# A state-space scan on one core: its two token tiles taken stage by stage in turn, one sum moved from GpSimd to VectorE, one product from VectorE to ScalarE

## The chip, the cores and the metric

The program runs on one core of a Trainium2 chip. Its time is device microseconds of one execution; of three runs of the kernel before the median is 2680.12 us (2672.77 to 2683.09). One execution was also recorded by the hardware profiler, and every row below comes from that one.

## What is computed

Four layers work on 256 context tokens and 256 latent tokens of width 1024: gated linear attention, a state-space mixer (SSD), an even attention mixer and an odd one, each followed by a feed-forward part (the last one a mixture of eight experts). The change is inside the SSD mixer, the second of the four. Cut to the scan, per group of four heads:

```
cum  = cumsum(dt * a)
seg  = cum[:, None] - cum[None, :]
decay = exp(where(mask, seg, -inf))
xdt  = xi * dt
cb   = einsum('bign,bjgn->bijg', ci, bi)
y    = einsum('bijg,bijgr,bjgrp->bigrp', cb, decay, xdt)
y    = y + einsum('bign,bigr,bgrpn->bigrp', ci, exp(cum), s)
```

It runs forwards and backwards over the tokens, the two results are added, `xs * d` is added, and the sum is multiplied by `silu(z)`. There are eight groups. The context's tokens only leave a state; results are wanted for the latents alone.

## The kernel before

Products are made in single precision from split operands: `split` (L419, L420) casts the upper bits on ScalarE and takes the rest on VectorE or GpSimd, and `mm3` (L441 to L443) makes three matmuls of each. A weight unit is loaded by DMA, split in halves of 1024 columns (`whi` on ScalarE at L419, `wlo` on VectorE at L420) and used by `gemm_ws`, where the weights stay and 512 or 256 tokens move.

`ssd` runs one group after another. `gemm(g)` makes the inputs of group g: two units of x (512 tokens each), B (512 tokens), C and two of z (256 tokens each). Each of the first four goes from PSUM through `conv` (L1193 and L1196 on ScalarE, four passes at L1198 on VectorE) into the tile `FZ`; z is copied there at L1212. `scan(g)` starts with SiLU over all of `FZ` (L1220, with a table load ahead of it), so it can't start before all of `gemm(g)` has been evacuated. Then, in steps that end at each `yield`:

- four steps that transpose the four token tiles (L1229), copy them out of PSUM (L1230, ScalarE) and scale x (L1233, VectorE);
- two steps, one per direction, that make the states (L1240, L1248 on TensorE; L1242 ScalarE; L1246, L1251 VectorE; L1250 GpSimd);
- five steps for latent tile 2 and then the same five for tile 3: C times B (L1258) and its two masked copies `gm` (L1262); `R`, a mask times the decay's exponent, as a high part on VectorE and a low part on GpSimd (both L1269), which TensorE sums to `pe` (L1274); `exp(pe)` on ScalarE (L1284), the step sizes times `gm` (`w4`, L1286 ScalarE, L1287 VectorE), and their product `e4` on GpSimd (L1288); the state's part `pi` (L1292), scaled on VectorE (L1294), its two directions added on GpSimd (L1296); last `py` (L1301 and L1304), which needs both that sum and `e4`, then L1307 on VectorE and the product with `silu(z)` on GpSimd (L1310);
- one step that squares the group's result (L1317, ScalarE) and adds it up (L1318, GpSimd).

That is 17 steps. `weave(scan(g), gemm(g + 1), *PACE[2])` takes 1.3 of the next group's gemm steps after each scan step, and what is left of them at the end; the last group is woven with the first products of w_out (`early`, `PACE[3]`, also 1.3). A gemm here has 18 steps (four per x unit, four for B, two for C, two per z unit). So 18 gemm steps are used up after 14 of the scan's 17.

The order on each engine is set when the program is built: a scheduler goes by the program's order, the buffers and its own estimates. Every engine then takes its instructions strictly in that order. Two kinds of buffers matter: `pat` holds two PSUM banks, used in turn for `pg` (C times B), `pe`, `pi` and `py`; `R` has three buffers, two of which one direction of one tile takes. `hc4` is scratch: `w4`, `e4`, and from column 1024 the state's part.

Of the kernel before, what the change touches and what calls it, by code (L numbers as in the profile page):

```python
# [22 lines left out]
# ---------------------------------------------------------------- host layout  # L23
# [43 lines left out]
def _ev_bias(rpb):  # L67
    """Relative position bias by query and key, with the column window's -1e30: [8, 128, 2 * 256]."""
# [22 lines left out]
def _col(v):  # L91
    """[n * 128] -> [128, n]."""
# [3 lines left out]
def _ada_tiles(L, c):  # L96
    """The feature tiles of the conditioning's group c; the first layer's shift and scale come in halves."""
# [39 lines left out]
def layout(inp):  # L137
    """The arrays the program takes; every one a rearrangement of an input or a constant."""
# [20 lines left out]
    # GLA  # L159
# [19 lines left out]
    # SSD  # L179
# [9 lines left out]
    # second block  # L189
# [55 lines left out]
    # constants of the shapes  # L245
# [24 lines left out]
# ---------------------------------------------------------------- the program  # L270
# [11 lines left out]
# steps of filler, and of the conditioning, per step of a phase's main part  # L282
PACE = (0.7, 0.3), (0.45, 0.6), (1.3, 0.3), (1.3, 0.6), (0.9, 0.5), (0.65, 0.5), (0.25, 0.3), (1.25, 0.5), (0.26, 0.3)
# [29 lines left out]
class Net:  # L313
# [10 lines left out]
    def banks(self, mm, tp, at=0, sc=0):  # L324
        """PSUM of a phase: accumulators, transposes, and two kinds for the mixers."""
# [62 lines left out]
    def open_h(self, es):  # L388
        """The residual, tokens on partitions: two tiles of the context, two of the latents."""
# [32 lines left out]
    def load(self, ap, n):  # L422
        """A unit of weights, split, in two halves: w(o, n) = parts of the columns o .. o + n."""
# [14 lines left out]
    def mm3(self, ps, a, b, first, last):  # L438
        """ps += a.T @ b."""
# [5 lines left out]
    def ws_acc(self, w, nm, m, x, t0, nt, ps):  # L445
        """Yields every 3072 columns or so."""
# [5 lines left out]
    def gemm_ws(self, ap, x, evac, nm=2, span=None):  # L452
        """Weights stationary: a unit of nm * 128 columns, tokens moving; evac(m, psum [columns, tokens])."""
# [8 lines left out]
    def gemm_ws_halves(self, units, x):  # L462
        """Several units at once, the context's tokens first: units = [(ap, nm, evac)]."""
# [14 lines left out]
    def gemm_xs(self, units, x, tts, n, evac, fill=0):  # L478
        """Tokens stationary: units = [(ap, ks)], each n columns of the weights of the k-tiles ks."""
# [22 lines left out]
    def unit(self, w, ks, x, pss, first, last, evac=None):  # L502
        """Part of a product with tokens stationary: pss = {token tile: psum}; w(k) the weights of k-tile k, split."""
# [8 lines left out]
    def flush(self):  # L512
        """What was put off until the tensor engine has other work behind it."""
# [1785 lines left out]
```

## Time and profile before

| | |
|---|---|
| median of 3 runs | 2680.12 us |
| the runs | 2672.77, 2683.09, 2680.12 us |
| span of the profiled execution | 2672.4 us |
| run nearest to that span | 2672.77 us, 0.4 us above it |
| TensorE, VectorE, ScalarE, GpSimd busy | 94%, 73%, 46%, 25% of the span |
| the eight scans | from about 831 to 1166 us |

The profiled execution's own time, as the device counts it, is not listed apart; its span agrees with the fastest run to 0.4 us, and 2672.8 us is used for it. A group's scan starts where its transposes (L1229) start: at 831.16, 873.39, 917.40, 963.05, 1007.60, 1052.23, 1097.19 and 1139.13 us. The seven stretches between them are called periods; what follows 1139.13 is the last group, without a next one to weave in. A granted clock of 1.00 is 2.4 GHz, 0.50 is 1.2 GHz.

### The profile page before, as it was taken

How to read it: one execution, taken by the hardware profiler on the slowest of the kernel's cores; microseconds unless marked ns; L12 is line 12 of the kernel's file. 1: busy time of each engine (PE TensorE's matmuls, PEld its weight loads, DVE VectorE, ACT ScalarE, POOL GpSimd, SP SyncE). 2: the span in 40 equal slices, each digit the busy share in tenths (PEclk: the TensorE clock that was granted, in tenths of full speed). 3: DMA queues.
4: the chain of work that ended last, by engine and by line, in shares of the span. 5: the costliest groups of instructions: out<-in, count | busy, mean ns of one | idle time of the engine just before them, and what ended most of it. 6: DMA issues, size and time to landing. Idle time of an engine off the chain costs nothing.

```text
span 2672.4 us, 38317 instructions
## 1 busy us (share of the span) xinstructions
PE 2524.6 (94%) x14350; PEld 2065.7 (77%) x14350; DVE 1962.1 (73%) x3015; ACT 1239.3 (46%) x1899; POOL 659.3 (25%) x533
## 2 busy tenths in 40 slices
PE   6999999999999989899999999999999898999998
PEld 3877668877777777778988877888888676888886
DVE  3566787799988777877566457756438776999987
ACT  2433444223246555545544344322225444878775
POOL 1122334032332333424224123112124431000000
PEclk8999999999999989998999999999999998999999
DMA  8334556665642222245553225555524125999995
GB/s 283 125 129 142 195 200 205 213 219 198 209 161 94 71 67 71 71 159 173 189 188 122 78 71 174 180 194 194 191 92 163 61 72 193 341 328 356 336 334 217
DMA packets 137506, 471.66 MB, mean 176 GB/s; under 512 B 16544, under 2 KB 21792, under 8 KB 137056
## 3 DMA queue, kind: packets, MB, share of 16 engines
q1 hardware_dynamic: 131264, 458.34, 50.8%
q10 hardware_dynamic: 6048, 10.80, 1.2%
q8 instruction: 115, 1.88, 0.3%
q14 instruction: 79, 0.65, 0.1%
HBM read 467.96 MB, written 1.11 MB: 176 GB/s over the span
## 4 chain that ended last, share of the span: by engine, by line
PE 52%; DVE 8%; issue 4%; POOL 3%; ACT 2%; DMA 0%; ACTq 0%; DVEq 0%; POOLq 0%
PE b L441 15%; PE b L443 15%; PE b L442 15%; DVE wlo L420 2%; DVE FZ L1198 1%; PE b L1396 1%; POOL hrs L1371 1%; POOL Hc L1296 1%; PE b L1427 1%; PE b L1415 1%; DVE R L1269 1%; PE b L1301 1%; ACT whi L419 1%; PE b L1930 1%; PE b L2007 1%
## 5 line engine op out<-in xcount | busy, mean ns | idle before, releaser
L419 ACT ACTIVATE whi<-wraw 128x1024 fp32r<-128x1024 f32 x472 | 491.9, 1047 | 582.4 <-PE b L443 246.6
L420 DVE TENSOR_TENSOR wlo<-wraw,whi 128x1024 fp32r<-128x1024 f32 x472 | 594.4, 1268 | 209.0 <-ACT whi L419 205.4
L441 PE MATMUL b<-whi,big 128*128 128x512 f32 (+1 forms) x1696 | 600.1, 355 | 5.6 <-DVE xn L1374 4.1
L442 PE MATMUL b<-wlo,big 128*128 128x512 f32 (+1 forms) x1696 | 591.1, 349 | 5.1 <-DVE wlo L420 5.1
L443 PE MATMUL b<-whi,big 128*128 128x512 f32 (+1 forms) x1696 | 589.4, 348 | 0.6 <-POOL big L420 0.5
L441 PE MATMUL b<-big,whi 128*128 128x512 f32 (+1 forms) x1512 | 548.4, 364 | 8.4 <-ACT big L419 5.7
L443 PE MATMUL b<-big,wlo 128*128 128x512 f32 (+1 forms) x1512 | 535.9, 355 | 7.4 <-DVE wlo L420 5.5
L442 PE MATMUL b<-big,whi 128*128 128x512 f32 (+1 forms) x1512 | 535.8, 355 | 2.3 <-POOL big L420 2.1
L441 PEld LDWEIGHTS b<-whi,big 128*128 128x128 f32 x1696 | 324.3, 191 | 56.9 <-issue 13.5
L442 PEld LDWEIGHTS b<-wlo,big 128*128 128x128 f32 x1696 | 324.4, 191 | 46.5 <-DVE wlo L420 9.2
L443 PEld LDWEIGHTS b<-whi,big 128*128 128x128 f32 x1696 | 324.1, 191 | 40.5 <-issue 2.0
L441 PEld LDWEIGHTS b<-big,whi 128*128 128x128 f32 x1512 | 295.0, 195 | 55.4 <-issue 9.6
L443 PEld LDWEIGHTS b<-big,wlo 128*128 128x128 f32 x1512 | 294.6, 195 | 46.2 <-DVE wlo L420 9.0
L442 PEld LDWEIGHTS b<-big,whi 128*128 128x128 f32 x1512 | 295.0, 195 | 40.5 <-POOL big L420 5.0
L559 DVE SCALAR_TENSOR_TENSOR aacc<-wraw,s,aacc 128x1024 f32<-128x1024 f32 x161 | 232.8, 1473 | 38.3 <-DMA wraw<-in_ada 37.9
L420 POOL TENSOR_TENSOR big<-ut,big 128x256 fp32r<-128x256 f32 x101 | 105.7, 1055 | 380.9 <-ACT big L419 380.1
L420 DVE TENSOR_TENSOR wlo<-big,whi 128x1024 fp32r<-128x1024 f32 (+1 forms) x157 | 184.6, 1197 | 18.1 <-ACT whi L419 15.5
L419 ACT ACTIVATE whi<-big 128x1024 fp32r<-128x1024 f32 (+1 forms) x157 | 160.5, 1034 | 33.8 <-PE b L443 26.6
L420 POOL TENSOR_TENSOR big<-hr,big 128x512 fp32r<-128x512 f32 (+1 forms) x64 | 85.1, 1330 | 344.1 <-ACT big L419 315.4
L1198 DVE SCALAR_TENSOR_TENSOR FZ<-xp,vecs,FZ 128x512 f32<-128x512 f32 (+1 forms) x128 | 99.9, 780 | 12.8 <-ACT FZ L1196 11.7
L419 ACT ACTIVATE big<-ut 128x256 fp32r<-128x256 f32 x156 | 62.3, 412 | 84.3 <-DVE ut L676 26.9
L761 DVE TENSOR_TENSOR yt<-b,gate 128x512 f32<-128x512 f32 x92 | 63.0, 685 | 25.2 <-PE b L443 25.0
(449 smaller groups left out, 3543.2 us busy)
## 6 DMA issues: line engine op xcount, KB each, us to landing
big<-in_moe SPq DMA_DIRECT2D x148, 512.0 KB, 6.4
wraw<-in_f SPq DMA_DIRECT2D x136, 512.0 KB, 4.0
wraw<-in_ada SPq DMA_DIRECT2D x120, 512.0 KB, 4.2
araw<-in_ada SPq DMA_DIRECT2D x72, 512.0 KB, 4.1
wraw<-in_moe SPq DMA_DIRECT2D x72, 512.0 KB, 6.3
wraw<-in_g SPq DMA_DIRECT2D x68, 512.0 KB, 3.8
Hc<-in_moe SPq DMA_DIRECT2D x36, 512.0 KB, 6.8
wraw<-in_gla_o SPq DMA_DIRECT2D x16, 512.0 KB
```

Source lines behind the costliest of these rows:

```text
L419: self.nc.scalar.activation(hi, t, AF.Copy)
L420: (eng or self.nc.gpsimd).tensor_tensor(lo, t, hi, op=OP.subtract)
L441: mm(ps, a[0], b[0], start=first, stop=False)
L442: mm(ps, a[0], b[1], start=False, stop=False)
L443: mm(ps, a[1], b[0], start=False, stop=last)
L559: nc.vector.scalar_tensor_tensor(acc[v], raw, s, acc[v], op0=OP.mult, op1=OP.add)
L761: nc.vector.tensor_mul(y, ps, gt)
L1198: V.scalar_tensor_tensor(o, xp[:, :ns, k:k + 256], w(k), o, op0=OP.mult, op1=OP.add)
L1269: (V if t is TH else nc.gpsimd).tensor_tensor(R[z, t is TL], tri["le" if z == 0 else "ge"][:, None, :].to_broadcast([128, 4, 128]), hc(t[: ...
L1296: nc.gpsimd.tensor_tensor(ys, ys, hc4[:, 1280:1536], op=OP.add)
L1301: mm(o, ys[:, 128 * i:128 * i + 128], self.ident, start=True, stop=False)
L1371: nc.gpsimd.tensor_tensor(r, ss, self.mhalf.to_broadcast([128, nh]), op=OP.pow)
```

## The change

The steps of the latents' tiles become functions: `begin` (C times B and `gm`), `spread` (R), `segments` (sums of R), `within` (`exp`, `w4`, `e4`), `before` (the state's part) and `both` (`py` and what follows). Tile 3's steps begin before tile 2's `both`; two empty steps stand ahead of tile 3's `both`. The number of steps stays 17. The state's part gets room of its own per tile. The two directions are added on VectorE, not GpSimd. R's high part is made by four copies on ScalarE, each with one head's column as its scale, not by one product on VectorE; its low part stays on GpSimd. `PACE[2]` goes from 1.3 to 1.1, `PACE[3]` from 1.3 to 1.2. Comments and docstrings are dropped, so line numbers move.

```diff
-PACE = (0.7, 0.3), (0.45, 0.6), (1.3, 0.3), (1.3, 0.6), ...
+PACE = (0.7, 0.3), (0.45, 0.6), (1.1, 0.3), (1.2, 0.6), ...
...
-                for t in (TH, TL):
-                    R[z, t is TL] = pool.tile([128, 4, 128], F32R, name="R", bufs=3)
-                    (V if t is TH else nc.gpsimd).tensor_tensor(
-                        R[z, t is TL], tri[...][:, None, :].to_broadcast([128, 4, 128]), hc(t[:, tt], z, 0, 128), op=OP.mult)
+                for i, t in enumerate((TH, TL)):
+                    R[tt, z, i] = pool.tile([128, 4, 128], F32R, name="R", bufs=3)
+                    if i:
+                        nc.gpsimd.tensor_tensor(R[tt, z, i], tri[n][:, None, :].to_broadcast([128, 4, 128]), hc(t[:, tt], z, 0, 128), op=OP.mult)
+                        continue
+                    for r in range(4):
+                        o = 32 * z + 4 * g + r
+                        nc.scalar.activation(R[tt, z, i][:, r, :], ahead[n], AF.Copy, scale=t.bitcast(F32)[:, tt, o:o + 1])
...
-                nc.gpsimd.tensor_tensor(ys, ys, hc4[:, 1280:1536], op=OP.add)
+                V.tensor_tensor(room[tt][:, 0:256], room[tt][:, 0:256], room[tt][:, 256:512], op=OP.add)
...
+            begin(2); spread(2, 0)
+            yield
+            before(2); segments(2, 0); spread(2, 1)
+            yield
+            segments(2, 1); within(2)
+            yield
+            begin(3); spread(3, 0)
+            yield
+            before(3); segments(3, 0); spread(3, 1)
+            yield
+            both(2)
+            yield
+            segments(3, 1); within(3)
+            yield
+            yield
+            yield
+            both(3)
+            yield
```

(The calls of one step, which stand on lines of their own, are put on one line here.)

Three places show what moves. The built order differs from before only inside the SSD mixer. The names: `b` is a PSUM bank, `Hc` is `hc4`, `S` a state, `tgt` and `tlt` the masks against which R is summed, `tle` and `tge` those that R is made of; after the change L1264 is C times B, L1298 the state's part, L1284 the sums of R, L1306 and L1309 `py`, L1299 the scaling of the state's part, L1300 its sum, L1291 the second half of `w4`, L1348 the square.

TensorE, tile 2 of the fourth group, from the state's part to `py`; at "..." stand only rows of L441 to L443 (18 matmuls in all). Before:

```order
L1292 MATMUL b<-S,FZ 128x256 x2
L441 MATMUL b<-big_6781,whi 128x512
...
L443 MATMUL b<-big_6781,wlo 128x256
L1301 MATMUL b<-ident,Hc 128x128
L1304 MATMUL b<-Hc,big_6956 64x128 x2
```

The same after the change; at "..." again only gemm rows, all 512 wide (6, 6, 12 and 6 of them):

```order
L1298 MATMUL b<-S,FZ 128x256 x2
L1284 MATMUL b<-R,tgt 128x512 x2
...
L1284 MATMUL b<-R,tlt 128x512 x2
...
L1264 MATMUL b<-FZ 128x128
...
L1298 MATMUL b<-S,FZ 128x256 x2
L1284 MATMUL b<-R,tgt 128x512 x2
...
L1306 MATMUL b<-ident,Hc 128x128
L1309 MATMUL b<-Hc,big_6956 64x128 x2
```

Between tile 2's state part and its `py` there were 18 gemm matmuls; there are now 30, three sums of R, and tile 3's C times B and state part. For tile 3 there were 8 gemm matmuls, 512 wide; there are now 6 that are 512 wide and 48 that are 256 wide, with tile 2's `py` and a sum of R among them.

VectorE, the same tile, from `gm` to the scaling of the state's part. Before:

```order
L1262 TENSOR_TENSOR gm<-b,tge 128x128
L1287 SCALAR_TENSOR_TENSOR Hc<-gm,T,Hc 128x128 x4
L420 TENSOR_TENSOR wlo<-wraw,whi 128x1024
L1198 SCALAR_TENSOR_TENSOR FZ<-xp,vecs,FZ 128x512
L1269 TENSOR_TENSOR R<-tle,TH 128x512
L1198 SCALAR_TENSOR_TENSOR FZ<-xp,vecs,FZ 128x512
L1269 TENSOR_TENSOR R<-tge,TH 128x512
L1198 SCALAR_TENSOR_TENSOR FZ<-xp,vecs,FZ 128x512
L1294 TENSOR_TENSOR Hc<-b,EX 128x512
```

After:

```order
L1267 TENSOR_TENSOR gm<-b,tge 128x128
L420 TENSOR_TENSOR wlo<-wraw,whi 128x1024
L1291 SCALAR_TENSOR_TENSOR Hc<-gm,T,Hc 128x128 x2
L1299 TENSOR_TENSOR Hc<-b,EX 128x512
L1291 SCALAR_TENSOR_TENSOR Hc<-gm,T,Hc 128x128
L1300 TENSOR_TENSOR Hc<-Hc 128x256
L1291 SCALAR_TENSOR_TENSOR Hc<-gm,T,Hc 128x128
```

Both R products and three passes of the convolution no longer stand ahead of the scaling, and the sum follows it on the same engine.

ScalarE, the end of a group, from the copy of its first z unit to the next group's SiLU and transposes. Before:

```order
L1212 ACTIVATE FZ<-b 128x256
L1284 ACTIVATE Hc<-b 128x512
L419 ACTIVATE whi<-wraw 128x1024 x2
L1212 ACTIVATE FZ<-b 128x256
L1220 ACT_TABLE_LOAD
L1220 ACTIVATE FZ<-FZ 128x2304
L1317 ACTIVATE Hc<-big_6904 128x512
L1230 ACTIVATE big_6956<-b 128x384 x4
```

After:

```order
L1212 ACTIVATE FZ<-b 128x256
L419 ACTIVATE whi<-wraw 128x1024
L1348 ACTIVATE Hc<-big_6904 128x512
L419 ACTIVATE whi<-wraw 128x1024
L1212 ACTIVATE FZ<-b 128x256
L1220 ACT_TABLE_LOAD
L1220 ACTIVATE FZ<-FZ 128x2304
L1230 ACTIVATE big_6956<-b 128x384 x3
```

The square of the group's result stood behind the next group's SiLU; it now stands ahead of the second z copy, the table load and that SiLU. On TensorE, 24 gemm matmuls of 256 columns (the second z unit) and 22 of 512 stand between tile 3's `py` and the next group's transposes; before, there were 8 of 512 ahead of tile 3's `py` and 6 behind it.

## Rows read from the trace of the kernel before

**Rows 1.** Busy time by stretch: the seven periods, then the last group.

```profile
core 0: us, PE busy (x) PEld busy (x) DVE busy (x) ACT busy (x) POOL busy (x), PEclk, DMA share, GB/s
831.16:1139.13 307.97, 274.72 (x1471) 230.62 (x1472) 240.17 (x406) 163.81 (x254) 114.22 (x89) 0.93 0.23 75
1139.13:1166.00 26.87, 24.24 (x107) 17.95 (x107) 22.29 (x40) 15.56 (x33) 12.51 (x12) 0.88 0.18 58
```

**Rows 2.** TensorE's waits in the seven periods: us in total, times, longest.

```profile
PE b L1301 <- POOL Hc L1296: 32.4, 14, 3.1
```

**Rows 3.** TensorE in order of time, third period: start, us, instruction, [idle before <-releaser].

```profile
929.73 0.39 PE L443 MATMUL b<-big,wlo 128*128 128x512 f32 x1
...
930.41 0.40 PE L443 MATMUL b<-big,wlo 128*128 128x512 f32 x1
...
936.59 0.28 PE L441 MATMUL b<-big,whi 128*128 128x256 f32 x1
...
937.90 0.28 PE L443 MATMUL b<-big,wlo 128*128 128x256 f32 x1
940.20 0.49 PE L1301 MATMUL b<-ident,Hc 128*128 128x128 f32 x2 [2.02 <-POOL Hc L1296]
...
957.63 0.59 PE L1301 MATMUL b<-ident,Hc 128*128 128x128 f32 x2 [3.13 <-POOL Hc L1296]
```

**Rows 4.** Busy time by microsecond after three idle stretches; columns as in rows 1.

```profile
941.00:942.00 1.00, 1.00 (x6) 0.69 (x6) 0.48 (x1) 0.00 (x0) 0.00 (x0) 0.50 0.00 0
...
963.00:964.00 1.00, 1.00 (x8) 1.00 (x6) 0.00 (x0) 0.27 (x1) 0.67 (x1) 0.50 0.00 0
...
1144.00:1145.00 1.00, 0.14 (x2) 0.13 (x2) 1.00 (x2) 1.00 (x5) 0.70 (x2) 1.00 0.00 0
1145.00:1146.00 1.00, 1.00 (x5) 0.86 (x6) 1.00 (x3) 1.00 (x4) 0.56 (x1) 1.00 0.00 0
```

**Rows 5.** VectorE in order of time, ahead of the first gap.

```profile
934.61 1.76 DVE L1269 TENSOR_TENSOR R<-tle,TH 128x512 fp32r<-128x512 f32 x1
...
938.22 0.68 DVE L1294 TENSOR_TENSOR Hc<-b,EX 128x512 f32<-128x512 f32 x1
```

**Rows 6.** GpSimd in order of time, ahead of the first gap.

```profile
939.05 1.10 POOL L1296 TENSOR_TENSOR Hc<-Hc 128x256 f32<-128x256 f32 x1 [3.22 <-DVE Hc L1294]
```

**Rows 7.** Groups of instructions, seven periods: busy us, mean ns, idle before, releaser.

```profile
L419 ACT ACTIVATE whi<-wraw 128x1024 fp32r<-128x1024 f32 x43 | 45.3, 1053 | 53.0 <-PE b L442 53.0
...
L1269 DVE TENSOR_TENSOR R<-tle,TH 128x512 fp32r<-128x512 f32 x14 | 23.5, 1681 | 0.0
...
L1296 POOL TENSOR_TENSOR Hc<-Hc 128x256 f32<-128x256 f32 x14 | 18.4, 1317 | 33.1 <-DVE Hc L1294 33.1
L1286 ACT ACTIVATE Hc<-gm,T 128x128 f32<-128x128 f32 x56 | 17.8, 389 | 16.8 <-DVE gm L1262 16.8
...
L1220 ACT ACTIVATE FZ<-FZ 128x2304 f32<-128x2304 f32 x7 | 14.9, 2123 | 0.1
L1310 POOL TENSOR_TENSOR big<-big,FZ 128x256 f32<-128x256 f32 x14 | 13.5, 965 | 42.0 <-DVE big L1307 42.0
L1269 DVE TENSOR_TENSOR R<-tge,TH 128x512 fp32r<-128x512 f32 x15 | 13.4, 891 | 0.0
...
L1307 DVE SCALAR_TENSOR_TENSOR big<-FZ,vecs,b 128x128 f32<-128x128 f32 x28 | 9.1, 345 | 14.0 <-PE b L1304 14.0
...
L1220 ACT ACT_TABLE_LOAD x7 | 9.0, 1283 | 0.1
...
L1251 DVE TENSOR_TENSOR S<-S,b 128x256 f32<-128x256 f32 x14 | 5.8, 414 | 3.5 <-POOL S L1250 3.5
L1212 ACT ACTIVATE FZ<-b 128x256 f32<-128x256 f32 x14 | 5.2, 375 | 6.6 <-PE b L443 6.6
L1317 ACT ACTIVATE Hc<-big 128x512 f32<-128x512 f32 x5 | 3.2, 630 | 20.0 <-POOL big L1310 20.0
```

More of the change, by code (lines that the diff above doesn't have):

```diff
@@ L1253, in scan @@
                 yield
-            for tt in (2, 3):
-                B = F[:, 1024 + 128 * tt:1152 + 128 * tt]
-                C = F[:, 1536 + 128 * (tt - 2):1664 + 128 * (tt - 2)]
+            gm, R, pe = {}, {}, {}
+            ahead = {"le": tri["le"].bitcast(F32), "ge": tri["ge"].bitcast(F32)}
+            C = {tt: F[:, 1536 + 128 * (tt - 2):1664 + 128 * (tt - 2)] for tt in (2, 3)}
+            room = {tt: hc4[:, 1024 + 512 * (tt - 2):1536 + 512 * (tt - 2)] for tt in (2, 3)}
+            w4 = hc4[:, 0:512].rearrange("p (r i) -> p r i", r=4)
@@ L1257, in scan, with begin @@
+            e4 = hc4[:, 512:1024].rearrange("p (r i) -> p r i", r=4)
+            def begin(tt):
                 pg = self.bank(self.pat)
-                mm(pg[:, :128], B, C, start=True, stop=True)
-                gm = []
+                mm(pg[:, :128], F[:, 1024 + 128 * tt:1152 + 128 * tt], C[tt], start=True, stop=True)
                 for n in ("le", "ge"):
-                    t = pool.tile([128, 128], F32, name="gm", bufs=3)
-                    V.tensor_mul(t, pg[:, :128], tri[n])
-                    gm.append(t)
@@ L1264, in scan @@
-                R = {}
-                def spread(z):
-                    for t in (TH, TL):
-                        R[z, t is TL] = pool.tile([128, 4, 128], F32R, name="R", bufs=3)
-                        (V if t is TH else nc.gpsimd).tensor_tensor(
-                            R[z, t is TL], tri["le" if z == 0 else "ge"][:, None, :].to_broadcast([128, 4, 128]), hc(t[:, tt], z, 0, 128), op=OP.mult)
-                def segments(z):
-                    for i in range(2):
-                        mm(pe, tri["gt" if z == 0 else "lt"], R[z, i].rearrange("p a b -> p (a b)"), start=z == i == 0, stop=z == i == 1)
@@ L1275, in scan @@
-                spread(0)
-                yield
-                pe = self.bank(self.pat)
-                segments(0)
-                spread(1)
-                yield
-                segments(1)
-                w4 = hc4[:, 0:512].rearrange("p (r i) -> p r i", r=4)
-                e4 = hc4[:, 512:1024].rearrange("p (r i) -> p r i", r=4)
-                nc.scalar.activation(hc4[:, 512:1024], pe, AF.Exp)
+                    gm[tt, n] = pool.tile([128, 128], F32, name="gm", bufs=3)
+                    V.tensor_mul(gm[tt, n], pg[:, :128], tri[n])
@@ new lines, in spread @@
+            def spread(tt, z):
+                n = "le" if z == 0 else "ge"
+                for i, t in enumerate((TH, TL)):
[6 more added lines that the diff above has]
+                        nc.scalar.activation(R[tt, z, i][:, r, :], ahead[n], AF.Copy, scale=t.bitcast(F32)[:, tt, o:o + 1])
@@ L1285, in scan, with segments, within @@
+            def segments(tt, z):
+                if z == 0:
+                    pe[tt] = self.bank(self.pat)
+                for i in range(2):
+                    mm(pe[tt], tri["gt" if z == 0 else "lt"], R[tt, z, i].rearrange("p a b -> p (a b)"), start=z == i == 0, stop=z == i == 1)
+            def within(tt):
+                nc.scalar.activation(hc4[:, 512:1024], pe[tt], AF.Exp)
                 for r in range(4):
-                    nc.scalar.activation(w4[:, r, :], gm[0], AF.Copy, scale=T[:, tt, 4 * g + r:4 * g + r + 1])
@@ L1310, in scan @@
                 nc.gpsimd.tensor_tensor(yy, yy, F[:, 1792:2304].rearrange("p (i t) -> p i t", i=2)[:, :, sl], op=OP.mult)
-                yield
+            begin(2)
+            spread(2, 0)
+            yield
+            before(2)
+            segments(2, 0)
+            spread(2, 1)
+            yield
+            segments(2, 1)
+            within(2)
+            yield
+            begin(3)
+            spread(3, 0)
+            yield
+            before(3)
+            segments(3, 0)
+            spread(3, 1)
+            yield
+            both(2)
+            yield
+            segments(3, 1)
+            within(3)
+            yield
[3 more added lines that the diff above has]
+            yield
             yy = Y[:, 2 * g:2 * g + 2, :].rearrange("p i t -> p (i t)")
```

17 lines of the change are left out of this document (8 added, 9 removed).

## The prediction

> **What bounds it now.** I began with the busy time of the stretch that the change touches. In the seven periods TensorE is busy 274.72 of 307.97 us, VectorE 240.17, ScalarE 163.81, GpSimd 114.22; the granted clock is 0.93 on average [rows 1]. So TensorE is the engine to look at, and it has two kinds of loss there. It is idle for 307.97 - 274.72 = 33.3 us. And while it works it is partly at 1.2 GHz: 307.97 x (1 - 0.93) = 21.6 us of full-speed work are lost to that (the clock is rounded, so 20 to 23). Without both, the periods would take 307.97 - 33.3 - 21.6 = 253.1 us, or 36.2 each where it is 44.0 now. That is the floor for everything below.
>
> Next I asked who ends the idle time. TensorE's waits have one entry that matters: 14 waits for the sum of the state's two directions on GpSimd (L1296), 32.4 us in all, two per period [rows 2]. In order of time they are one gap of about 2.0 us and one of about 3.1 us in a period [rows 3]. The gap is not GpSimd's slowness alone: L1296 itself had been waiting 3.22 us for L1294 on VectorE [rows 6], and L1294 stood behind R and convolution passes in VectorE's queue; that R took 1.76 us [rows 5]. So the chain is VectorE's backlog, then 1.1 us or more of GpSimd, then TensorE.
>
> Last, the clock. After the gap of 2.02 us it stood at 0.50 for three whole microseconds, of which the first is shown; with the parts at either end 1.7 us of work is lost. After the gap of 3.13 us it was six whole ones, of which the last is shown, and 3.4 us lost. After a stop of 0.86 us in the last group the clock stayed at 1.00 [rows 4]. So a gap of 2 us costs about 3.7, one of 3.1 about 6.5, and a stop under 1 us costs itself. What the change must do is not to speed up an engine but to keep each stop below a microsecond.
>
> **The change part by part.**
>
> *Tile 3 between tile 2's steps, and `both` late.* No instruction more or less on TensorE. Between tile 2's state part and its `py` there now stand 30 gemm matmuls of 512 columns, at (930.41 - 929.73) / 3 = 0.227 us each, 6.8 us, plus three sums of R and tile 3's own small products, together some 9 us. For tile 3 it is 6 of these (1.4 us) and 48 of 256 columns at (937.90 - 936.59) / 11 = 0.119 us (5.7 us), over 7 us before tile 2's `py` is counted [rows 3]. Scaling and summing on VectorE need 0.68 us [rows 5] and about 0.41 us [rows 7], and the queue ahead of them is shorter. Both gaps should go: **-32.4 us** of idle time, and with it the low clock, **-21.6 us**.
>
> *The sum on VectorE.* No row shows a VectorE addition of this shape with both inputs in scratch; the same size with one input in PSUM (L1251) takes 0.414 us, the sum on GpSimd 1.317 [rows 7]. I take 0.41, being the same engine and size; 1.32 is the far end. Twice per period that is 0.8 us (up to 2.6), off the path, since the sum has several us of cover.
>
> *R's high part on ScalarE.* VectorE loses 23.5 + 13.4 = 36.9 us in the seven periods, 5.3 per period. ScalarE gets 16 copies of 128x128 per period. The nearest row, a scaled copy of that size, has a mean of 0.389 us [rows 7], so 6.2 us per period at most; less if back-to-back ones overlap, none less than zero. ScalarE then works 163.81 / 7 + 6.2 = 29.6 us of a 36.2 us period, VectorE 240.17 / 7 - 5.3 + 0.8 = 29.8, or 31.6 at the far end [rows 1, 7]. Both fit, with 82% and 82 to 87%. R is made a step ahead, so its copies cost nothing on the path as long as ScalarE keeps up. The Trainium skill (ScalarE: Activation LUTs, Rules for kernel authors) advises against this part: multiplications belong on VectorE, not ScalarE. Here the product on VectorE took 1.681 and 0.891 us on average for the two directions [rows 7], not clearly less than four copies at 0.389; by the trace the move is about even in engine time, and it pays only because VectorE is the engine that is late. By the page's advice it would be a loss, which is the last rival below.
>
> *The pace.* 18 gemm steps at 1.1 last through 16.4 of the 17 scan steps, not 14: the same matmuls, spread as cover to the end. Zero by itself.
>
> *What is late next.* I walked one new period in the built order with the durations above. Two places are tight.
> First, the next group's SiLU. ScalarE now squares the group's result ahead of the second z copy. From the end of tile 3's `py`: two VectorE passes with a convolution pass between them, about 1.1 us (0.345 each for the two), GpSimd's product 0.965, the square 0.630, a `whi` cast 1.053, the z copy 0.375, a table load 1.283, SiLU 2.123 [rows 7]: 7.5 us. TensorE has 24 matmuls of 0.119 and 22 of 0.227 in that time: 7.9 us [rows 3]. The margin is 0.4 us, and any disturbance uses it up; I put 0.5 us per period there.
> Second, tile 2's `py` takes the PSUM bank of tile 3's `pi`, which is free only after VectorE's scaling of tile 3. That stands behind a `w4` row, which waits for ScalarE's, which waits for tile 2's `e4` on GpSimd. In the walk this comes 0 to 0.7 us after TensorE; I put 0.7.
> Together 1.2 us in each of seven periods, **+8.4 us**, in stops too short to bring the clock down.
>
> *The last group* has little gemm to weave in either order. Now it has 26.87 - 24.24 = 2.6 us idle and 26.87 x 0.12 = 3.2 us lost to the clock [rows 1]. I take 0: all of it, 6 us, could go; and its SiLU has only 24 x 0.119 + 5 x 0.227 = 4.0 us of cover against the 7.5, so 3.5 us could be added.
>
> **The sum.** -32.4 - 21.6 + 8.4 + 0 = -45.6 us. The profiled execution ran about 2672.8 us, so it would be 2627.2. It is the fastest of the runs shown, 7.3 us under their median; against the median it is 2680.1 - 45.6 = **2634.5 us**, which I give.
>
> **The rivals.**
> *One stall comes back.* A stop of the shorter kind, 2.0 us idle and 1.7 us lost, appears once per period at the next group's transposes or at tile 2's `py`. For it: margins of 0.4 us and of nothing, and three engines above 80%. Against: VectorE drops 5 us of work per period. It gives 7 x 3.7 = 25.9 us in place of 8.4: 2680.1 - 54.0 + 25.9 = 2652.0. With the longer kind, 6.5 us, it is 7 x 6.5 = 45.5: 2671.6, near no change.
> *All of it goes.* No new stop, and the last group gains too: 2680.1 - 33.3 - 21.6 - 6 = 2619.2; a run as far under the median as the profiled one would show 2612.
> *Nothing moves.* That the change doesn't do what it says is excluded for the order, which is built; but the time stays if `py` is late for another reason than the sum, for its second input `e4`. Against: `e4` was not what the 14 waits ended on [rows 2]. It has the price of the longer stall above, 2671.6.
> *Slower: ScalarE's queue.* ScalarE takes its work in order. An R copy waits for the R buffer that TensorE's sums free, the square for GpSimd; behind them stand `whi` casts, on which VectorE's `wlo` and so the gemm depend, and the evacuations of PSUM. If each wait holds that queue for over 3 us, TensorE stops twice per period for the longer kind: 36.2 + 2 x 6.5 = 49.2 us where it was 44.0, 7 x 5.2 = 36 us more, 2716. It turns from gain to loss when the stops with their clock cost more than 44.0 - 36.2 = 7.8 us per period. Against: ScalarE's `whi` casts now wait 53.0 us in the periods for matmuls that free their buffers [rows 7], so they run with time in hand.
>
> **How the numbers follow.** A change of about 0.5%, 13.4 us, is what a measurement of this kernel can tell from none. Forecast (2622 to 2645): 0.57. One stall back (2645 to 2666): 0.24. All goes, under 2622: 0.06. Nothing moves (2667 to 2693): 0.08. Slower: 0.05. That is faster 0.87, same 0.08, slower 0.05. The range is 2612 to 2660: its lower end is the floor with the last group's gain in a run like the profiled one, which also takes in the lower end of the copies' cost; its upper end takes in most of the case with one short stall, and leaves out the long one, no change and the loss.
>
> **What would show it.** Right: TensorE's waits no longer list the sum; the scan's periods are 36 to 38 us; the granted clock in them is 0.98 or more; VectorE near 30 and ScalarE near 29 us per period. Wrong in the size: a wait at the transposes for SiLU, or at `py` for `e4` or for the scaling on VectorE, over 1.5 us long and followed by 0.50 clock. Wrong altogether: TensorE waiting for `wlo` or for R, with ScalarE busy to the end of each period.

## The result

The changed kernel takes 2650.81 us (median of four runs, 2645.45 to 2652.77); the kernel before, run beside it, 2681.61 (2672.77 to 2687.16). The ratio is 0.9886 with a 95% interval of 0.9864 to 0.9907: faster by 1.1%, 30.8 us by the medians, where 45.6 were forecast. By the medians the time is 16.3 us above the forecast, within the range. It lies in the band that the prediction gave to its first rival, one stall that comes back (2645 to 2666, chance 0.24), not in the forecast's own. The profiled execution took 2649.63 us, its span is 2647.8.

The profiled pair is compared from here on: spans of 2672.4 and 2647.8 us, 24.6 less. Nearly all of it lies in the seven periods.

### Profile after: stretches and waits

Busy time by stretch, after, columns as in rows 1: the seven periods, the last group, then the third and fourth period, and single microseconds behind the stops that open these two.

```profile
831.69:1116.42 284.73, 263.53 (x1470) 219.88 (x1471) 218.33 (x390) 193.19 (x367) 89.47 (x76) 0.97 0.26 83
1116.42:1143.00 26.58, 24.21 (x119) 18.00 (x120) 22.67 (x44) 19.10 (x45) 11.59 (x10) 1.00 0.19 69
...
911.81:951.80 39.99, 37.27 (x212) 30.85 (x213) 30.96 (x56) 27.20 (x52) 13.14 (x11) 1.00 0.25 80
951.80:992.87 41.07, 38.39 (x213) 32.27 (x213) 31.24 (x56) 27.56 (x52) 12.69 (x11) 0.96 0.25 78
...
912.00:913.00 1.00, 0.98 (x8) 0.67 (x8) 0.08 (x1) 0.60 (x2) 0.00 (x0) 1.00 0.47 193
913.00:914.00 1.00, 1.00 (x7) 0.74 (x7) 1.00 (x2) 0.74 (x3) 0.00 (x0) 1.00 0.00 0
...
952.00:953.00 1.00, 1.00 (x7) 0.91 (x6) 0.09 (x1) 0.53 (x2) 0.00 (x0) 0.64 0.45 180
953.00:954.00 1.00, 1.00 (x5) 0.96 (x5) 1.00 (x2) 0.45 (x1) 0.00 (x0) 0.50 0.00 0
```

Beside [rows 1], the seven periods went from 307.97 to 284.73 us, 23.2 less. TensorE's idle time fell from 33.3 to 284.73 - 263.53 = 21.2, its busy time from 274.72 to 263.53. The granted clock rose only from 0.93 to 0.97. VectorE lost 22 us of work, ScalarE gained 29.

TensorE's waits from the first group's transposes to the last group, after: us in total, times, longest.

```profile
PE b L1229 <- ACT FZ L1220: 11.8, 8, 1.9
PE b L1306 <- DVE Hc L1299: 5.8, 7, 0.8
PE b L441 <- ACT big L1364: 3.7, 1, 3.7
```

The wait for the sum [rows 2], 32.4 us, is gone from the list. Three others stand in its place: the next group's transposes wait for SiLU, 1.9 us at a time; tile 2's `py` waits for the scaling on VectorE, 5.8 / 7 = 0.83 us each; and once, ahead of the last group, the first product of w_out waits 3.7 us for ScalarE. They make up the 21.2 us.

TensorE in order of time, after: two of the stops for SiLU (start, us, instruction, [idle before <-releaser]).

```profile
911.81 0.87 PE L1229 MATMUL b<-ident,FZ 128*128 128x128 f32 x6 [1.85 <-ACT FZ L1220]
...
951.80 1.12 PE L1229 MATMUL b<-ident,FZ 128*128 128x128 f32 x6 [1.86 <-ACT FZ L1220]
```

After the first the clock stayed at 1.00, after the second it was at 0.64 and then 0.50, as after the gaps of [rows 4]. The stops are the same to 0.01 us. The first three periods run at 1.00 and take 40.0 us, the next three at 0.96 and take 41.1, the last at 0.92 and takes 41.4.

### Profile after: why SiLU is late

One stretch in order of time, after, all engines: from tile 3's `py` in the second period to the next group's SiLU.

```profile
901.13 1.21 DVE L420 TENSOR_TENSOR wlo<-wraw,whi 128x1024 fp32r<-128x1024 f32 x1
...
901.44 0.44 PE L1309 MATMUL b<-Hc,big 128*64 128x128 f32 x4
902.26 0.47 DVE L1198 SCALAR_TENSOR_TENSOR FZ<-xp,vecs,FZ 128x256 f32<-128x256 f32 x1
...
902.77 1.01 DVE L1198 SCALAR_TENSOR_TENSOR FZ<-xp,vecs,FZ 128x256 f32<-128x256 f32 x2
903.69 0.34 DVE L1312 SCALAR_TENSOR_TENSOR big<-FZ,vecs,b 128x128 f32<-128x128 f32 x1
903.95 0.48 DVE L1198 SCALAR_TENSOR_TENSOR FZ<-xp,vecs,FZ 128x256 f32<-128x256 f32 x1
904.35 0.34 DVE L1312 SCALAR_TENSOR_TENSOR big<-FZ,vecs,b 128x128 f32<-128x128 f32 x1
...
904.63 1.22 DVE L420 TENSOR_TENSOR wlo<-wraw,whi 128x1024 fp32r<-128x1024 f32 x1
...
904.77 1.67 POOL L1315 TENSOR_TENSOR big<-big,FZ 128x256 f32<-128x256 f32 x1 [5.91 <-DVE xp L1192]
...
906.47 0.64 ACT L1348 ACTIVATE Hc<-big 128x512 f32<-128x512 f32 x1 [1.99 <-POOL big L1315]
907.01 1.05 ACT L419 ACTIVATE whi<-wraw 128x1024 fp32r<-128x1024 f32 x1
...
907.96 0.36 ACT L1212 ACTIVATE FZ<-b 128x256 f32<-128x256 f32 x1
...
908.34 1.28 ACT L1220 ACT_TABLE_LOAD   x1
909.64 2.12 ACT L1220 ACTIVATE FZ<-FZ 128x2304 f32<-128x2304 f32 x1
```

`py` ends at 901.88. VectorE finishes the second L1312 only at 904.69, since a `wlo` split and four convolution passes stand ahead of it. GpSimd's product then takes 1.67 us, beside another split that VectorE began 0.14 us earlier; ScalarE sits idle 1.99 us for it, with the `whi` cast, the z copy, the table load and SiLU queued behind the square. SiLU ends at 911.76, TensorE goes on at 911.81.

The 3.7 us at w_out have the same origin: in ScalarE's queue L1364 starts at 1112.44, behind the z copy, a `whi` cast and the square, and the square starts at 1110.69 after a wait of 1.87 us for GpSimd's product.

The parts that were priced, in groups of the seven periods, after: busy us, mean ns, idle before.

```profile
L1315 POOL TENSOR_TENSOR big<-big,FZ 128x256 f32<-128x256 f32 x14 | 20.0, 1428 | 66.3 <-DVE xp L1192 35.5 <-DVE big L1312 30.8
...
L1278 ACT ACTIVATE R<-tge,TH 128x128 fp32r<-128x128 f32 x56 | 18.5, 391 | 0.0
...
L1300 DVE TENSOR_TENSOR Hc<-Hc 128x256 f32<-128x256 f32 x14 | 5.8, 412 | 0.0
```

R's copies (0.391 us) and the sum on VectorE (0.412) came as priced from [rows 7]; the product, 0.965 before, did not.

### The profile page after: what moved, and what is told of

Its sections match the earlier page's. It is cut to its first block, busy times and chain, and to the rows that moved or that the text cites. A ratio compares the mean times of both kernels' runs of the same rounds, so it can differ in the third digit from the quotient of the medians.

```text
span 2647.8 us, 38382 instructions
## 1 busy us (share of the span) xinstructions
PE 2509.8 (95%) x14350; PEld 2052.2 (78%) x14350; DVE 1939.2 (73%) x2999; ACT 1273.6 (48%) x2027; POOL 632.1 (24%) x517
## 5 line engine op out<-in xcount | busy, mean ns | idle before, releaser
L441 PE MATMUL b<-whi,big 128*128 128x512 f32 (+1 forms) x1696 | 599.6, 355 | 9.6 <-DVE xn L1405 4.4
L443 PE MATMUL b<-whi,big 128*128 128x512 f32 (+1 forms) x1696 | 588.9, 347 | 0.6 <-POOL big L420 0.5
L441 PE MATMUL b<-big,whi 128*128 128x512 f32 (+1 forms) x1512 | 540.2, 359 | 8.7 <-ACT big L419 5.7
L443 PE MATMUL b<-big,wlo 128*128 128x512 f32 (+1 forms) x1512 | 531.0, 352 | 6.5 <-DVE wlo L420 6.5
L442 PE MATMUL b<-big,whi 128*128 128x512 f32 (+1 forms) x1512 | 532.4, 352 | 2.4 <-POOL big L420 2.2
L441 PEld LDWEIGHTS b<-whi,big 128*128 128x128 f32 x1696 | 323.6, 191 | 61.7 <-issue 14.4
L443 PEld LDWEIGHTS b<-whi,big 128*128 128x128 f32 x1696 | 323.6, 191 | 40.3 <-issue 1.8
L441 PEld LDWEIGHTS b<-big,whi 128*128 128x128 f32 x1512 | 290.2, 192 | 56.2 <-issue 10.4
L443 PEld LDWEIGHTS b<-big,wlo 128*128 128x128 f32 x1512 | 290.8, 193 | 43.9 <-DVE wlo L420 8.2
L442 PEld LDWEIGHTS b<-big,whi 128*128 128x128 f32 x1512 | 291.1, 193 | 39.6 <-POOL big L420 5.0
L1198 DVE SCALAR_TENSOR_TENSOR FZ<-xp,vecs,FZ 128x512 f32<-128x512 f32 (+1 forms) x128 | 110.8, 866 | 11.3 <-ACT FZ L1196 10.1
```

Source lines behind the costliest of these rows:

```text
L441: mm(ps, a[0], b[0], start=first, stop=False)
L442: mm(ps, a[0], b[1], start=False, stop=False)
L443: mm(ps, a[1], b[0], start=False, stop=last)
L1198: V.scalar_tensor_tensor(o, xp[:, :ns, k:k + 256], w(k), o, op0=OP.mult, op1=OP.add)
```

## The experiments

Twelve kernels, each run four or five times beside the kernel before, on the same chip; the ratio given is against that. The first question was which of the remaining waits costs what; the second, which part of the change earns the gain.

### 1. The square on GpSimd

```diff
-                nc.scalar.activation(hc4[:, 0:512], yy, AF.Square)
+                nc.gpsimd.tensor_tensor(hc4[:, 0:512], yy, yy, op=OP.mult)
```

> The changed kernel with the square of each group's result on GpSimd, not on ScalarE; TensorE's order stays as it is. Theory (the SiLU of the next group is late because ScalarE stands at the square, which waits for GpSimd's product and so for VectorE's backlog): TensorE's waits at the transposes, 11.8 us in all and 1.9 each in the changed kernel, fall under 2 us in all; the granted clock of the seven periods goes from 0.97 to 0.99 or more; the periods are 38 to 38.5 us where they are 40 to 41; the time falls by 12 to 18 us against the changed kernel, to a ratio of 0.982 to 0.984 against the kernel before. Rival (SiLU is late by VectorE's convolution passes, the square is beside the point): waits of 1.2 us or more per period stay, the time moves by less than 5 us, ratio 0.987 to 0.989.

Measured: 2631.51 us, ratio 0.9829 (0.9812 to 0.9846). TensorE's waits:

```profile
PE b L1306 <- DVE Hc L1299: 5.4, 7, 0.8
...
PE b L1229 <- ACT FZ L1220: 0.4, 2, 0.2
```

The seven periods, columns as in rows 1:

```profile
832.84:1098.31 265.47, 257.13 (x1471) 213.65 (x1471) 218.22 (x390) 188.15 (x360) 102.56 (x83) 1.00 0.26 88
```

The wait for SiLU is gone, and the low clock with it: 284.73 - 265.47 = 19.3 us less. So it was the square's place in ScalarE's queue that held SiLU up.

### 2. Tile 2's `py` in another bank

```diff
-                py = self.bank(self.pat)
+                py = self.bank(self.ptp if tt == 2 else self.pat)
```

> The changed kernel with tile 2's py in a bank of the transposes' pool (two banks, idle then), not in the pool of pi; nothing else. Theory (TensorE waits 0.82 us per period at tile 2's py for the bank that tile 3's pi still holds until VectorE has scaled it): these waits, 5.8 us in all, go, and nothing takes their place; 4 to 7 us less than the changed kernel, ratio 0.9865 or so. Rival (e4 of tile 2 is as late as the bank): the wait turns into one for GpSimd's e4 of nearly the same length, under 2 us gained.

Measured: 2648.47 us, ratio 0.9900 (0.9882 to 0.9918). TensorE's waits:

```profile
PE b L1229 <- ACT FZ L1220: 16.1, 8, 2.6
```

A miss. The wait at `py`, 0.83 us, went, but the one for SiLU grew by 0.70 us, from 1.86 to 2.56, and now every such stop is followed by low clock (0.95 in the seven periods). The time at which SiLU ends is set by VectorE's backlog and ScalarE's queue, not by TensorE; getting there sooner is only waiting longer.

### 3. Both edits

The edits of the first two together.

> Both edits together, square on GpSimd and tile 2's py in a bank of its own. Theory (the two waits are apart, and with them gone nothing else stands on TensorE's way in the periods): TensorE idle under 6 us in the seven periods, clock 0.99 or 1.00, periods of 37.3 to 37.8 us; 18 to 24 us less than the changed kernel, ratio 0.979 to 0.982. Rival (VectorE, at 31 of 37 us, turns up as the next wait at once): gains do not add, under 14 us.

Measured: 2623.14 us, ratio 0.9807 (0.9792 to 0.9822). The seven periods:

```profile
826.59:1084.72 258.13, 254.67 (x1470) 213.92 (x1470) 217.24 (x390) 188.37 (x360) 103.61 (x83) 1.00 0.27 90
```

With SiLU out of the way the bank is worth 265.47 - 258.13 = 7.3 us more, of which 5.4 are the waits. TensorE is busy for all but 3.5 us of seven periods of 36.9.

### 4. R's high part back on VectorE

```diff
-                    for r in range(4):
-                        o = 32 * z + 4 * g + r
-                        nc.scalar.activation(R[tt, z, i][:, r, :], ahead[n], AF.Copy, scale=...)
+                    (nc.gpsimd if i else V).tensor_tensor(R[tt, z, i], tri[n]..., hc(t[:, tt], z, 0, 128), op=OP.mult)
```

> The changed kernel with R's high part on VectorE again, one product per direction and tile, as in the kernel before; TensorE's order is that of the changed kernel. Theory (VectorE is the engine that is late, and the move of R takes 5 us of its work per period away): VectorE's work per period goes from 31 to 36 us, tile 2's py waits for it by 2 us or more per period with the clock falling behind it, and SiLU comes later too; 15 to 30 us more than the changed kernel, ratio 0.994 to 1.000. Rival (the order alone does it, the engine of R does not matter as long as R is made ahead): within 5 us of the changed kernel.

Measured: 2642.91 us, ratio 0.9874 (0.9856 to 0.9893). TensorE's waits:

```profile
PE b L1229 <- ACT FZ L1220: 10.1, 8, 1.5
PE b L1301 <- DVE Hc L1294: 7.0, 7, 1.0
```

The rival was right: VectorE works 240.51 of 280.16 us, 3.2 us more per period than in the changed kernel and not 5, and the waits hardly change (1.5 us for SiLU where it was 1.86, 1.0 for `py` where it was 0.83). Against the change as it stands, moving R to ScalarE gains nothing.

### 5. The old pace

```diff
-PACE = ..., (1.1, 0.3), (1.2, 0.6), ...
+PACE = ..., (1.3, 0.3), (1.3, 0.6), ...
```

> The changed kernel with both paces back at 1.3. In its built order the square stands behind the next group's SiLU again, as in the kernel before, and tile 3's py stands behind the last z matmuls with 18 gemm matmuls of 512 columns after it. Theory (the slower pace is what put the square ahead of SiLU, and that square is what makes SiLU late): waits for SiLU under 2 us in all, against 11.8; 8 to 17 us less than the changed kernel, ratio 0.982 to 0.986. Rival (the slower pace gives cover that tile 3's py needs): waits at tile 3's py for e4 or the sum take its place, 1 us or more per period; same as the changed kernel or slower, ratio 0.988 to 0.995.

Measured: 2630.72 us, ratio 0.9825 (0.9812 to 0.9839). TensorE's waits:

```profile
PE b L1306 <- DVE Hc L1299: 4.7, 7, 0.7
...
PE b L1229 <- ACT FZ L1220: 0.2, 1, 0.2
```

The seven periods:

```profile
829.55:1092.78 263.23, 256.01 (x1470) 214.38 (x1471) 223.97 (x390) 193.94 (x365) 89.07 (x75) 1.00 0.26 86
```

A pace of 1.3 takes more gemm steps per scan step than 1.1, so the old pace is the faster one. With it the scheduler puts the square behind the next group's SiLU again, as before the change, and SiLU's wait is gone without moving the square. Beside the whole change's 0.9886 the new pace costs 0.6%, some 16 us.

### 6. The order of steps alone

R back on VectorE, the sum back on GpSimd, the new pace:

```diff
+                    (nc.gpsimd if i else V).tensor_tensor(R[tt, z, i], tri[n]..., hc(t[:, tt], z, 0, 128), op=OP.mult)
...
-                V.tensor_tensor(room[tt][:, 0:256], room[tt][:, 0:256], room[tt][:, 256:512], op=OP.add)
+                nc.gpsimd.tensor_tensor(room[tt][:, 0:256], room[tt][:, 0:256], room[tt][:, 256:512], op=OP.add)
```

> The changed kernel with both engine moves undone: R's high part on VectorE, the sum of the directions on GpSimd; only the order of the steps and the paces are new. Theory (the order alone makes the gain, since the sum has several us of cover either way and py's wait ends on the scaling): the same as with only R moved back, ratio 0.986 to 0.990, the wait at tile 2's py ends on VectorE's scaling or on the sum and is 1 to 2 us. Rival (the sum's engine matters): it ends on GpSimd's sum, 2 us or more per period with the clock falling behind it, 10 us or more over the kernel with only R moved back, ratio 0.991 or above.

Measured: 2651.17 us, ratio 0.9899 (0.9883 to 0.9914), the interval overlapping that of the whole change (0.9864 to 0.9907). SiLU is waited for 14.0 us (2.22 at a time), `py` 7.1. So with the new pace the two engine moves are worth nothing that can be measured.

### 7. The engine moves alone

The kernel before with R's copies on ScalarE and the sum on VectorE, in the old order and at the old pace:

```diff
-                        (V if t is TH else nc.gpsimd).tensor_tensor(R[z, t is TL], ...)
+                        if t is TL:
+                            nc.gpsimd.tensor_tensor(R[z, True], ...)
+                            continue
+                        for r in range(4):
+                            nc.scalar.activation(R[z, False][:, r, :], tri[n].bitcast(F32), AF.Copy, scale=...)
...
-                nc.gpsimd.tensor_tensor(ys, ys, hc4[:, 1280:1536], op=OP.add)
+                V.tensor_tensor(ys, ys, hc4[:, 1280:1536], op=OP.add)
```

> The kernel before with only the two engine moves: R's high part on ScalarE, the sum on VectorE; the order of the steps and the paces are the old ones. Theory (two causes of the old gaps: VectorE's queue ahead of the scaling, and the short distance between state part and py): the gap at tile 2's py, 2.0 us, goes, that of tile 3, 3.1 us, shrinks to 1 to 2 us; 8 to 20 us less than the kernel before, ratio 0.992 to 0.997. Rival (the distance alone is the cause): both gaps stay above 1.5 us, ratio 0.998 to 1.002. Second rival (the engines alone are the cause): both gaps go, ratio under 0.989.

Measured: 2644.78 us, ratio 0.9878 (0.9863 to 0.9893); the seven periods take 279.43 us with the clock at 0.98. The gap at each `py` shrank, to 1.1 us for tile 2 and about 1.65 for tile 3, but stayed. A miss: the gaps lie between what the theory and its first rival expected, while the time is the one given for the second rival, whose gaps were to go. What is left of them ends on VectorE: tile 3's `py` at 907.39 follows the sum, which ran from 906.84 to 907.25 behind a `wlo` split. (Most are put down to ScalarE's `whi` and SiLU, which end at about that time and which `py` doesn't read.) The result is as good as the whole change, but that has another pace. At the old pace the two parts can be compared: the order alone gives 0.9908 (tenth experiment), the engine moves alone 0.9878, both together 0.9825 (fifth).

### 8. Both edits, and R on VectorE

The third and the fourth experiment together: square on GpSimd, bank for `py`, R back on VectorE.

> The version with the square on GpSimd and tile 2's py in a bank of its own, with R's high part on VectorE instead of ScalarE. Theory (with the two waits gone TensorE is the bound at 36.8 us per period, and VectorE with 34 to 36 us of work has no room left): VectorE becomes late, waits for wlo or for conv's result in SiLU appear; 5 us or more slower than the version without this edit, ratio above 0.9825. Rival (R is made ahead, and VectorE at 94% still keeps up): within 4 us of it, ratio 0.979 to 0.982.

Measured: 2624.76 us, ratio 0.9800 (0.9786 to 0.9813), like the third. The rival was right. VectorE works 243.12 of 258.54 us, and TensorE waits for it only once, 1.6 us at w_out: 94% busy was no bound here, since its work was not late.

### 9. The old pace and the bank

> The changed kernel with both paces back at 1.3 and tile 2's py in a bank of the transposes' pool; the square stays on ScalarE. Theory (the wait for the bank, 0.67 us per period with the old pace, is the last one in the periods, and SiLU has time in hand, so that nothing is given back this time): periods of 36.8 to 37.1 us, 3 to 6 us less than with the old pace alone, ratio 0.979 to 0.982, the same as the square on GpSimd with the bank of its own. Rival (as with the bank alone at the new pace): the wait turns up again at the transposes or at tile 3's py, ratio 0.982 to 0.984.

Measured: 2638.16 us, ratio 0.9850 (0.9832 to 0.9868). A miss, and not better than the old pace alone. In some periods tile 3's `py` waits for `e4` on GpSimd, 9.0 us in four waits. GpSimd and VectorE in order of time ahead of the one at 906.90:

```profile
899.93 0.48 DVE L1198 SCALAR_TENSOR_TENSOR FZ<-xp,vecs,FZ 128x256 f32<-128x256 f32 x1
900.09 3.37 POOL L1315 TENSOR_TENSOR big<-big,FZ 128x256 f32<-128x256 f32 x1 [4.33 <-DVE big L1312]
...
901.64 1.22 DVE L420 TENSOR_TENSOR wlo<-wraw,whi 128x1024 fp32r<-128x1024 f32 x1
902.78 0.96 DVE L1198 SCALAR_TENSOR_TENSOR FZ<-xp,vecs,FZ 128x256 f32<-128x256 f32 x1
```

GpSimd's product, 0.91 us at the median, is open for 3.37 us while VectorE goes from one instruction to the next without a pause. R's low part and `e4` stand behind it, and `e4`, 1.36 us at the median, takes 2.24 itself.

### 10. The old pace, order alone

R on VectorE and the sum on GpSimd, as in the sixth experiment, at the old pace.

> The changed kernel with both paces back at 1.3, R's high part back on VectorE and the sum back on GpSimd, so that only the order of the latents' steps is new against the kernel before. Theory (the order is the whole gain; the engine moves take work off an engine that is not late): ratio 0.981 to 0.985, as with the old pace alone, and waits at tile 2's py for VectorE's scaling of about 1 us per period. Rival (the engine moves are worth something once the square is out of the way): waits at py of 2 us or more with the clock falling, ratio 0.987 or above.

Measured: 2656.64 us, ratio 0.9908 (0.9894 to 0.9923). A miss. TensorE's waits:

```profile
PE b L1301 <- DVE Hc L1294: 11.9, 7, 2.0
PE b L1279 <- DVE xp L1192: 9.5, 7, 1.4
```

Here VectorE is late twice in a period. The second wait is put down to a memset (L1192), but ends with the copies `gm` (L1267), which free a bank 0.05 us earlier; R, 1.76 us long there, stands ahead of them. Against 0.9825 with the engine moves (fifth experiment) they are worth 0.8%, so it depends on the pace whether they earn anything.

### 11. Tile 2's product on VectorE

On the ninth:

```diff
-                nc.gpsimd.tensor_tensor(yy, yy, F[:, 1792:2304]..., op=OP.mult)
+                (V if tt == 2 else nc.gpsimd).tensor_tensor(yy, yy, F[:, 1792:2304]..., op=OP.mult)
```

> The version with the old pace and tile 2's py in a bank of its own, with tile 2's product with silu(z) on VectorE instead of GpSimd. Theory (in that version GpSimd's product of tile 2 was held up to 3.37 us while VectorE ran on without a break, tile 3's e4 stood behind it in GpSimd's queue, and TensorE waited for e4): the waits for e4, 9.0 us in all, fall under 2 us, no product on GpSimd is over 1.7 us, 6 to 14 us less than without this edit, ratio 0.979 to 0.983. Rival (e4 is late by VectorE's half of w4 or by the exponential): the waits for e4 stay above 5 us in all, ratio 0.984 to 0.987.

Measured: 2645.58 us, ratio 0.9882 (0.9866 to 0.9899). A miss: seven waits for `e4`, 17.7 us. In order of time:

```profile
898.51 3.62 POOL L1292 TENSOR_TENSOR Hc<-Hc 128x512 f32<-128x512 f32 x1 [2.10 <-DVE Hc L1291]
898.66 2.35 DVE L420 TENSOR_TENSOR wlo<-wraw,whi 128x1024 fp32r<-128x1024 f32 x2
...
900.98 2.23 DVE L420 TENSOR_TENSOR wlo<-wraw,whi 128x1024 fp32r<-128x1024 f32 x1
```

With the product gone, `e4` itself is held up: 3.62 us, beside two `wlo` splits of 1.2 us each, and the third split takes 2.23. It starts late by VectorE's half of `w4`, as the rival had it, but with the ninth experiment's median of 1.36 us it would have ended at 899.87, while TensorE's `py` began at 899.60 and waited until 902.19. So it is not one operation that is slow: the product there and `e4` here were held up beside unbroken VectorE work.

### 12. `e4` on VectorE

On the ninth:

```diff
-                nc.gpsimd.tensor_tensor(e4, e4, w4, op=OP.mult)
+                V.tensor_tensor(e4, e4, w4, op=OP.mult)
```

> The kernel of e9 (the change with the slower pace of before and tile 2's py in a bank of its own) with one edit: e4, the copy of the exponentials that GpSimd made (L1292), is made by VectorE. Theory: what is left in e9 is a GpSimd operation that is held up while VectorE runs on without a break (e4 took 3.6 us in e11 where its median is 1.4, the product 3.4 in e9 where its median is 0.9); with e4 gone from GpSimd the only operations left there that something waits for are the sums' neighbours and the product, waits for e4 are gone, waits of TensorE for GpSimd stay under 2 us in seven periods, VectorE gains some 0.6 to 0.7 us per tile that has one, the period is 37 us, ratio 0.978 to 0.982. Rival: the product is held up in its place, or VectorE, busier by the same amount, is itself late for py or for SiLU; waits of over 1 us per period by TensorE for VectorE, ScalarE or GpSimd at py or at the next transposes, ratio 0.984 or above.

Measured: 2620.14 us, ratio 0.9784 (0.9764 to 0.9803). The seven periods:

```profile
829.81:1086.36 256.55, 254.34 (x1471) 213.83 (x1471) 210.01 (x404) 193.60 (x366) 81.82 (x61) 1.00 0.27 89
```

(The "slower pace of before" in the expectation is 1.3.) No wait of TensorE for `e4` is left, the periods take 36.65 us on average, and TensorE is idle for 2.2 us of all seven. This kernel, with the third and the eighth, is the fastest of the study; their intervals overlap. Groups of VectorE's instructions in the ninth, from 830 to 1110 us:

```profile
L420 DVE TENSOR_TENSOR wlo<-wraw,whi 128x1024 fp32r<-128x1024 f32 x45 | 64.2, 1448 | 9.5 <-ACT whi L419 9.5
...
L1300 DVE TENSOR_TENSOR Hc<-Hc 128x256 f32<-128x256 f32 x14 | 13.5, 963 | 0.0
...
L1299 DVE TENSOR_TENSOR Hc<-b,EX 128x512 f32<-128x512 f32 x14 | 9.5, 678 | 0.0
```

and here, in the periods:

```profile
L420 DVE TENSOR_TENSOR wlo<-wraw,whi 128x1024 fp32r<-128x1024 f32 x43 | 52.8, 1246 | 9.5 <-ACT whi L419 9.5
...
L1292 DVE TENSOR_TENSOR Hc<-Hc 128x512 f32<-128x512 f32 x14 | 9.6, 683 | 0.0
L1299 DVE TENSOR_TENSOR Hc<-b,EX 128x512 f32<-128x512 f32 x14 | 9.5, 681 | 0.0
...
L1300 DVE TENSOR_TENSOR Hc<-Hc 128x256 f32<-128x256 f32 x14 | 5.8, 413 | 0.0
```

VectorE took over 9.6 us of work and is busy for less, 210.01 us where it was 222.66. The split and the sum, both of whose inputs are scratch, went from 1.448 to 1.246 and from 0.963 to 0.413 us; the scaling, which reads PSUM, did not change.

## Why the prediction was right in kind and off in size

**The gaps at `py`: right.** -32.4 us of idle came true in full; the sum is on no list of waits any more. But the new order is not the whole cause: the engine moves alone, in the old order, shortened the same gaps to 1.1 and 1.65 us, and at the old pace the order alone gains 0.9%, the engine moves alone 1.2% and both 1.75% (0.9908, 0.9878 and 0.9825).

**SiLU: the mechanism right, the size wrong, and with it the sum.** The place was named, the chain too, and its cover of 7.9 us came out at 911.81 - 1.85 - 901.88 = 8.1. The step that failed is "7.5 us ... the margin is 0.4 us ... I put 0.5 us per period". The chain took 911.76 - 901.88 = 9.9 us. VectorE's part, put at 1.1 us, took 904.69 - 901.88 = 2.8, because convolution passes and a split stood ahead of L1312 in its queue: its own duration and one pass were counted, the backlog wasn't. GpSimd's product, put at 0.965, took 1.67, since it started beside a split. The rest, put at 5.5, took 5.3. The stop was 1.86 us, not 0.5: 11.8 us, not 3.5.

**The clock: -21.6 us forecast, a little over half of it realised.** It rested on "stops too short to bring the clock down", and so fell with the step above. 284.73 x (1 - 0.97) = 8.5 us are still lost, by the rounded clock; busy time fell by 11.2 us. Some 1.6 us of the loss follow the stop at w_out, after which the clock is 0.50 from 1113 to 1116 us. The floor under it was nearly right: 36.2 us per period were reckoned, 36.65 were reached in the last experiment. Once the stop goes, so does the rest of the lost clock (first, fifth and last experiment: 1.00).

**The bank of `py`: right in place and size.** 0.7 us per period was put, 0.83 measured. The chain was another: in the second period VectorE runs without a break from 888.07 to the scaling at 891.73, and what stands ahead there are convolution passes, one of them 1.52 us, not a wait for ScalarE. What was not seen is that beside a longer stop behind it it costs nothing: taken away alone it came back at SiLU (second experiment).

**The last group: 0 put, -0.3 measured**, but the first product of w_out, ahead of it, waits 3.7 us for ScalarE (L1364) where it waited 0.8; that wait was not foreseen. The square ahead of it has a part in that: 1.7 us are left with the square on GpSimd, 0.3 in the last experiment.

Together, in the profiled pair: 11.9 us more idle than forecast and 10.4 less won back from the clock. These 22 us are the miss there; by medians it is 16, as the profiled execution of before was the fastest of its kernel's runs.

**"Zero by itself" for the pace: wrong.** No instruction is added, as was said, but the pace helps to decide where the scheduler puts the square. Spread to the end of the scan, the gemm's z copy and the SiLU behind it come later, and the square gets ahead of them. That took 0.6%, some 16 us, of the 2677.98 - 2630.72 = 47 us that the change gains without it.

**R on ScalarE "pays only because VectorE is the engine that is late": half right.** With the new pace it pays nothing (fourth, sixth and eighth experiments): with R on VectorE the stop at SiLU is 1.5 us where it is 1.86 with R on ScalarE, and VectorE at 94% holds TensorE up only once, at w_out. With the old pace the two engine moves together pay 0.8%; each alone was not tried there. Nor was the move "about even in engine time": R's 1.681 us on VectorE, the mean of one direction, is mostly 1.74 to 1.76 us beside `e4` on GpSimd. Where no GpSimd instruction ran beside it, R took 0.68 us, in the kernel before (936.96) as in the fourth experiment. Four copies on ScalarE take 1.27 us back to back. So VectorE was relieved of 3.2 us per period, not 5.3, and part of its backlog before was R held up beside `e4`.

**The rivals.** One stall coming back is what happened, at the place named first, with a shorter low clock: a stop of 1.86 us ahead of six periods, low clock behind four. That its 2652 is met to 1 us is partly luck: by its terms 14.9 us would be idle and 11.9 us lost to the clock, and 21.2 and 8.5 were measured. Of the signs given, the one for "wrong in the size" came: a wait for SiLU over 1.5 us, followed by 0.50 clock; the periods (40 to 41.4 us) and the clock (0.97) missed what was given for "right". Nothing moves fell. Of the slower queue on ScalarE one half is true, the square that waits for GpSimd with the rest of the queue behind it; the loss is not, as TensorE never waits for `wlo` or for R's copies in the seven periods.

## What to carry to other kernels

When a step is moved, follow the chain that it now ends in through every queue it crosses, and count what stands ahead in each queue, not only the step's own durations; here a margin of 0.4 us over a chain of eight instructions on three engines was none. A parameter that only spreads work can decide which of two instructions an in-order engine gets first: compare the built order at each setting. And a wait that stands ahead of a longer one was not worth removing until the longer one was gone. A mean over rows in which an instruction ran alone and rows in which it was held up prices neither: R's 1.681 us was 0.68 or 1.76.

## What the hardware showed that was not expected

The same stop does not always bring the clock down. Of the changed kernel's six stops of 1.85 to 1.86 us two left the clock at 1.00, and after four it stood at 0.50 for a while, with 212 to 214 matmuls in the period ahead of each; in the sixth experiment stops of 2.22 us were followed by periods at 0.96 (41.63 us, from 914.88) and at 1.00 (40.52 us, from 956.51). What decides it is not settled. After stops of 1.5 us (fourth experiment) the clock of the periods stayed at 1.00; it fell only behind the 4.5 us wait at w_out, which makes the 0.99 on average. After all six of 2.55 to 2.58 us (second experiment) it fell, some 1.5 us after TensorE had gone on.

GpSimd and VectorE hold each other up, where the operation on VectorE has both inputs in scratch. In the ninth experiment the sum of the directions takes 0.41 us in the seven places where no GpSimd instruction runs beside it, and 1.51 or 1.52 us in the seven where `e4` had started just ahead of it (its mean is 0.96). One of these, in order of time:

```profile
890.44 1.30 POOL L1292 TENSOR_TENSOR Hc<-Hc 128x512 f32<-128x512 f32 x1 [0.42 <-POOL R L1274]
890.49 1.52 DVE L1300 TENSOR_TENSOR Hc<-Hc 128x256 f32<-128x256 f32 x1
```

`e4` takes its usual time and the sum ends 0.27 us after it. In the chain for SiLU it is the other way round: the split began first and kept its 1.22 us, the product took 1.67. VectorE's scaling, with one input in PSUM, takes 0.68 us in every kernel, also in the seven places of the ninth experiment where it runs beside R's low part on GpSimd.

The Trainium skill (SBUF — State Buffer, SBUF: two separate sides) says that a VectorE operation with two inputs in SBUF and a GpSimd operation that reads SBUF share a pair of ports, and that whichever starts first has it for its whole instruction while the other blocks. These rows agree. Two others differ in how long: the product of the ninth experiment was open for 3.37 us, over several VectorE instructions, and `e4` at 898.51 in the eleventh for 3.62, over two `wlo` splits. In both VectorE's next instruction starts before the last one has ended; that GpSimd finds no opening for this reason is not shown.
